# One decoder layer on one core: the last down product and norms token-major, sums in idle work space, steps in a new order

## The chip, the core and the metric

The kernel runs on one core of a Trainium2 chip. Five engines with queues of their own work side by side: TensorE (PE, its weight loads PEld), VectorE (DVE), ScalarE (ACT), GpSimd (POOL) and SyncE (SP), which issues most transfers. Each takes its instructions in the order in which they stand in its queue and waits there for semaphores. The metric is the device time of one execution, in microseconds (us); lower is better.

## The reference

One layer of a hybrid decoder on 1024 prompt tokens and 32 sample tokens (T = 1056), width D = 1024, all in float32:

```python
proj = x @ w_in                                   # split among four head groups
...
mix = jnp.concatenate([o_a, o_b, o_c, o_d], axis=-1) @ w_o
x = layer_norm(ALPHA * x + mix, ln1_g, ln1_b)
x = layer_norm(ALPHA * x + memory_attention(x, mem_k, mem_v, w_xq, w_xo), ln2_g, ln2_b)
ffn = (jax.nn.silu(x @ w_gate) * (x @ w_up)) @ w_down
x = layer_norm(ALPHA * x + ffn, ln3_g, ln3_b)
```

The feed-forward width is 2816, that is 22 tiles of 128 or 11 pairs. Besides x the layer returns new caches and states, which the change does not touch. The change lies in the feed-forward part and the last norm.

## The kernel before, in words

**Numbers.** A float32 product is made of three passes in a faster type: each factor is split into a high part (a ScalarE cast, L206) and a low part (the difference, on VectorE or GpSimd, L214), and `mm3` (L198 to L202) adds high·high, high·low and low·high. Names end in h and l for the two parts: `Xh`, `Xl` are the input, `wh`, `wl` a weight, `dh`, `dl` a down weight, `hh`, `hl` or `he` the product silu(gate)·up. The weights' parts of gate and up live in rings of two buffers, `WH` and `WL`. Raw weights arrive by transfers of 512 KB into `rw`. Many smaller tiles share general slots, taken by `H(...)` and returned by `free(...)`.

**Layout.** Activations are feature-major: `M` has 128 features by 8 tiles by 1056 tokens. Products go to PSUM tiles, `PM` (3 buffers, pm) and `PSB` (5 buffers, ps).

**Feed-forward.** The tokens go in two halves, 0 to 512 and 512 to 1056 (`PART`; widths 256+256 and 272+272). Some pairs of the first half are run early, beside cross-attention (`ff_early`). For the others each pair has seven products in place of eight (`products`, L1624): sums of weight quarters (`sc`, `s4` in the tile `work`) and of token quarters, which `sums_a` makes for the first half and `sums_b` (L1593) for the second. `half_gate`, `half_up` and `half_down` each yield after a product or a group, and `play(ORDER..., streams)` interleaves them: one letter is one step of that stream. `half_down(hf, p)` loads two down weights, then has 16 groups (8 feature tiles by 2 token ranges) of 6 matmuls, each drained by a VectorE add into `M` (L1744). The first pair of the second half is run without sums (`gate_up(ff, PART[1])`), and `sums_b()` follows it.

**Last norm.** `finish(i)` (L1756) takes a block of 128 tokens (block 8: the 32 sample tokens): 8 transposes of `M` to token-major PSUM (`tp`, L220), `bn_stats` (L1765) and `bn_aggr` (L1766), subtraction of the mean and gain (L1772), `rsqrt` (L222: a logarithm, an exponential and one step of refinement), then by mode either a VectorE row that scales and adds the bias (mode 0, L1781) or a ScalarE scale and a GpSimd add (mode 1, L1787), then the store (L1789). Blocks 0 to 3 run beside pairs 1 to 4 of the second half, blocks 4 to 8 at the very end beside the down product of the last pair, in which the token ranges come in the order 784-1056, 640-784, 512-640.

**Tables.** ScalarE's Silu and its Exp/Ln lie in different function tables. `act` (L152) puts an explicit load (L156) ahead of an Exp or Ln, behind the last Silu recorded; where the queue comes out otherwise, the compiler adds a load at L159 or L160.

**Order.** The program is recorded in the order of the code and the strings, and then a scheduler with a timeline model orders each engine's queue. So a string moves instructions only in part; the rows below show what came out.

Of the kernel before, what the change touches and what calls it, by code (L numbers as in the profile page):

```python
# [91 lines left out]
def build(ctx: ExitStack, tc: tile.TileContext, A):  # L92
# [58 lines left out]

    def act(out, in_, func, **kw):  # L152
        if func in (AF.Exp, AF.Ln):
            if table["set"] != "ln_exp":
                with tc.issue_after(table["last"]) if table["last"] else nullcontext():
                    table["load"] = S.preload_act_table_set("natural_log_exp_and_others").ins  # L156
                table["set"] = "ln_exp"
            with tc.issue_after(table["load"]):
                return S.activation(out, in_, func, **kw)  # L159
# [59 lines left out]
    def tp(out, in_, n=P):  # L219
        PE.transpose(out, in_, ident[:n, :n])  # L220

    def rsqrt(y, v, eps, t):  # L222

        V.tensor_scalar(t, v, eps, None, ALU.add)
# [4 lines left out]
        V.scalar_tensor_tensor(y, t, 1.5, y, ALU.add, ALU.mult)
# [1363 lines left out]
    def sums_b():  # L1593

        (a0, a1), (b0, b1) = PART[1]
        places = [lambda t, i: t[:, 2 * i:2 * i + 2, b0:b1], lambda t, i: t[:, 2 * i:2 * i + 2, 0:272],
                  lambda t, i: t[:, 4 + 2 * i:6 + 2 * i, 0:272],
                  lambda t, i: t[:, 4 * i:4 * i + 4, 272:408].rearrange("p (k s) n -> p k s n", s=2)]
        for i in range(2):
# [4 lines left out]
            V.tensor_tensor(t2, M[:, j, b0:b1], t1, ALU.subtract)  # L1604
            V.tensor_tensor(t4, M[:, j, a0:a1], t2, ALU.subtract)
            for n, (x, e) in enumerate(((t1, V), (t2, V), (t3, G), (t4, V))):
                h, l = places[n](Xh, i), places[n](Xl, i)
                if n == 3:
                    x = x.rearrange("p k (s n) -> p k s n", s=2)
                S.copy(h, x)  # L1610
                e.tensor_tensor(l, x, h.bitcast(F32), ALU.subtract)
            free(t1, t2, t3, t4)
# [81 lines left out]
    def half_up(hf, p):
        if p - 1 in downs[hf]:
            need(f"d{hf}.{p - 1}")
        sl = sil_of(hf)
# [8 lines left out]

        def hl(m):
            S.copy(hs[m][0], sl[:, m])
# [47 lines left out]
    def finish(i):  # L1756

        gb = gbt[0]
        n = P if i < 8 else NB * TS
        st, ag = SM([P, 2, 6], s="fst", tag="fst", bufs=2), SM([P, 5], s="fag", tag="fag", bufs=2)  # L1760
        pss = [PM(), PM()] if CFG['fpm'] and i >= 4 else [PSB(), PSB()]
        for hf in range(2):
            for f in range(4):
# [1 line left out]
            V.bn_stats(st[:n, hf], pss[hf][:n])  # L1765
        V.bn_aggr(ag[:n, 0:2], st[:n])  # L1766
        y = H([P, D], s="y")
        hs = [slice(0, 512), slice(512, D)]
        mode = CFG['fin'].get(i, 0)
        if mode < 2:  # L1770
            for hf in range(2):
                V.scalar_tensor_tensor(y[:n, hs[hf]], pss[hf][:n], ag[:n, 0:1], gb[0][:n, hs[hf]], ALU.subtract, ALU.mult)  # L1772
# [86 lines left out]
```

## Time and profile before

| what | value |
|---|---|
| time, median of 3 runs | 1430.63 us (1429.28 to 3872.03) |
| the profiled execution, its time | 1430.61 us |
| its span (first to last instruction) | 1428.8 us |
| mean granted TensorE clock | 0.973 |
| HBM read, written | 125.32 MB, 6.78 MB |

The 40 slices of the span, each digit the busy share in tenths:

```profile
PE   6999999998998998799999999999899999999995
...
DVE  6704658589667768687487999887688898888866
ACT  4424753432556758666346443443434553343334
POOL 5222452364000001022052000001400000000001
PEclk9999999999899999899999999999999999999997
```

TensorE is nearly full in all but the first and the last slice, about 36 us each. The slices near 28 (1000 to 1036 us) hold the first pair of the second half, the last two the tail. A row of a timeline has the start in us, the duration in us, the engine, line, operation, tiles and shape, and in brackets the idle time of that engine just before and what ended it. A row of a wait has total us, number and longest.

### The profile page before, as it was taken

Reading aid. Unit: us, or ns where it says so; the run is one execution under the profiler, and the core shown is the slowest. Engines: PE = TensorE matmul, PEld = TensorE weight load, DVE = VectorE, ACT = ScalarE, POOL = GpSimd, SP = SyncE. Lnnn points to the kernel's source line nnn. Section 1 sums busy time; section 2 is a strip of 40 time slices with the busy share of each in tenths; the row PEclk is TensorE's granted clock in tenths of the full one; section 3 lists DMA queues with packets and bytes.
Section 4 is the critical chain, followed back from the end, with each engine's and each line's share of the span. In section 5 each row is a group of like instructions: output and inputs, shape, how many; then the busy total and the mean of one; then the engine's idle time right before and its main releaser. Section 6 shows DMA issues by size and latency. Waiting matters only on the chain.

```text
span 1428.8 us, 25133 instructions
## 1 busy us (share of the span) xinstructions
PE 1345.6 (94%) x10065; PEld 1279.2 (90%) x10065; DVE 1077.6 (75%) x1972; ACT 670.0 (47%) x1147; POOL 236.4 (17%) x164
## 2 busy tenths in 40 slices
PE   6999999998998998799999999999899999999995
PEld 5998888997897997688799999999799998999995
DVE  6704658589667768687487999887688898888866
ACT  4424753432556758666346443443434553343334
POOL 5222452364000001022052000001400000000001
PEclk9999999999899999899999999999999999999997
DMA  9201111110253445143422333332333333333311
GB/s 301 77 21 41 31 30 50 47 40 24 75 163 104 148 119 151 49 126 119 133 60 68 110 104 104 90 118 75 111 97 91 102 104 112 100 100 90 104 60 63
DMA packets 188447, 132.61 MB, mean 93 GB/s; under 512 B 14573, under 2 KB 177618, under 8 KB 188306
## 3 DMA queue, kind: packets, MB, share of 16 engines
q1 hardware_dynamic: 187225, 128.27, 29.9%
q0 software_dynamic: 928, 2.67, 0.6%
q8 instruction: 79, 1.29, 0.4%
q14 instruction: 39, 0.31, 0.1%
q10 hardware_dynamic: 176, 0.07, 0.0%
HBM read 125.32 MB, written 6.78 MB: 92 GB/s over the span
## 4 chain that ended last, share of the span: by engine, by line
PE 41%; DVE 7%; DMA 4%; ACT 3%; issue 2%; POOL 0%; DVEq 0%; ACTq 0%; POOLq 0%; SPq 0%
PE ps L199 7%; PE ps L202 7%; PE ps L200 7%; PE pm L199 6%; PE pm L200 6%; PE pm L202 6%; DMA rw<-in_w_gate 2%; DVE wl L214 1%; DMA rw<-in_w_up 1%; PE ps L1313 1%; ACT L159 1%; ACT dh L206 1%; DMA rw<-in_w_down 0%; PE ps L1358 0%; DVE M L1481 0%
## 5 line engine op out<-in xcount | busy, mean ns | idle before, releaser
L199 PE MATMUL pm<-Xh,wh 128*128 128x256 f32 (+3 forms) x944 | 270.6, 310 | 14.7 <-ACT Xh L1133 9.8
L200 PE MATMUL pm<-Xl,wh 128*128 128x256 f32 (+3 forms) x944 | 267.2, 306 | 3.4 <-DVE Xl L1134 1.9
L206 ACT CAST wh<-rw 128x1024 fp32r<-128x1024 f32 x145 | 151.8, 1050 | 154.0 <-PE pm L200 43.7
L199 PEld LDWEIGHTS pm<-Xh,wh 128*128 128x128 f32 x944 | 180.8, 192 | 21.5 <-ACT Xh L1133 11.4
L214 DVE TENSOR_TENSOR wl<-rw,wh 128x1024 fp32r<-128x1024 f32 x122 | 152.8, 1254 | 49.3 <-ACT wh L206 46.3
L200 PEld LDWEIGHTS pm<-Xl,wh 128*128 128x128 f32 x944 | 180.7, 192 | 7.2 <-issue 2.5
L202 PE MATMUL pm<-Xh,wl 128*128 128x256 f32 (+3 forms) x944 | 159.4, 305 | 0.0
L202 PEld LDWEIGHTS pm<-Xh,wl 128*128 128x128 f32 x944 | 139.7, 191 | 1.5 <-issue 1.2
L199 PE MATMUL ps<-hh,dh 128*128 128x272 f32 (+3 forms) x370 | 99.9, 291 | 15.3 <-ACT dh L206 8.1
L214 POOL TENSOR_TENSOR wl<-rw,wh 128x1024 fp32r<-128x1024 f32 x23 | 57.1, 2482 | 287.0 <-ACT wh L206 269.3
L200 PE MATMUL ps<-hh,dh 128*128 128x272 f32 (+3 forms) x370 | 99.1, 286 | 0.0
L199 PEld LDWEIGHTS ps<-hh,dh 128*128 128x128 f32 x370 | 70.2, 191 | 17.4 <-ACT dh L206 8.6
L206 ACT CAST dh<-rw 128x1024 fp32r<-128x1024 f32 x44 | 45.9, 1047 | 82.1 <-PE ps L202 27.0
L1744 DVE TENSOR_TENSOR M<-M,ps 128x272 f32<-128x272 f32 (+3 forms) x175 | 69.7, 412 | 12.4 <-PE ps L202 12.0
L199 PE MATMUL ps<-Xh,wh 128*128 128x272 f32 (+1 forms) x296 | 76.5, 287 | 0.0
L200 PE MATMUL ps<-Xl,wh 128*128 128x272 f32 (+1 forms) x296 | 76.4, 287 | 0.0
L202 PE MATMUL ps<-hh,dl 128*128 128x272 f32 (+3 forms) x370 | 75.8, 285 | 0.0
L200 PEld LDWEIGHTS ps<-hh,dh 128*128 128x128 f32 x370 | 70.2, 190 | 0.4 <-DVE hh L1709 0.4
L199 PE MATMUL pm<-mixh,wh 128*128 128x256 f32 (+1 forms) x256 | 65.9, 291 | 0.2 <-ACT mixh L160 0.2
L200 PE MATMUL pm<-mixl,wh 128*128 128x256 f32 (+1 forms) x256 | 65.4, 289 | 0.2 <-DVE mixl L1168 0.2
L199 PE MATMUL pm<-hh,dh 128*128 128x272 f32 (+3 forms) x222 | 60.8, 291 | 3.8 <-DVE y L1772 2.3
L206 ACT CAST g<-work 128x1024 fp32r<-128x1024 f32 x34 | 35.7, 1049 | 60.1 <-PE pm L200 26.2
(454 smaller groups left out, 3668.9 us busy)
## 6 DMA issues: line engine op xcount, KB each, us to landing
rw<-in_w_gate SPq DMA_DIRECT2D x45, 512.0 KB
rw<-in_w_up SPq DMA_DIRECT2D x44, 512.0 KB
rw<-in_w_down SPq DMA_DIRECT2D x44, 512.0 KB
rw<-in_w_o SPq DMA_DIRECT2D x23, 384.0 KB
rw<-in_w_in SPq DMA_DIRECT2D x15, 512.0 KB
xraw<-in_x_prompt SPq DMA_DIRECT2D x8, 512.0 KB
out_y_prompt<-y SPq DMA_DIRECT2D x8, 512.0 KB
vreg<-in_w_o SPq DMA_DIRECT2D x9, 384.0 KB
```

The lines of the kernel that those rows point to most:

```text
L159: return S.activation(out, in_, func, **kw)
L199: PE.matmul(out, wh(k), xh(k), start=(start and k == 0), stop=False)
L200: PE.matmul(out, wh(k), xl(k), start=False, stop=False)
L202: i = PE.matmul(out, wl(k), xh(k), start=False, stop=(k == nk - 1))
L206: S.copy(hi, raw)
L214: (e or G).tensor_tensor(lo, raw, hi.bitcast(F32), ALU.subtract)
L1313: PE.matmul(sc_ps[r0:r0 + 64, :256], zq[:, 2 * b + ft], kx[:, b - b0, ft], start=(b % 4 == 0 and ft == 0), stop=(b % 4 == 3 and ft == 1))
L1744: V.tensor_tensor(z, z, ps, ALU.add)
```

## The change

1. **Tail.** The down product of the last pair is no longer run feature-major. `finish(4)` to `finish(8)` compute it token-major, with the hidden activations as the stationary and the down weight, 512 wide, as the moving operand, and add `M` itself by four plain float32 matmuls with the identity in place of the four transposes. Per block that is 2 × (6 + 4) matmuls. The 144 matmuls and 24 adds of the old product and 40 transposes go; 60 matmuls 512 wide and 40 of the identity come. The weights are loaded and split at the end of the last `play` ("w"), into the ring `WH`/`WL`. The order is 4, 5, 6, 7, 8; modes of 4 and 5 change from 0 to 1, of 8 from 1 to 0. The sample output is stored in two halves on two queues.
2. **rsqrt** is cut in two: the sum and the two ScalarE functions stand ahead of the gain rows in `finish`, the refinement behind.
3. **Tables.** The explicit load comes behind the last four Silu recorded, not the last one.
4. **sums_b.** Its temporaries lie in idle parts of `work` instead of four general slots at a time, all its VectorE and GpSimd rows are on VectorE, and it runs in three steps between the tiles of the pair without sums. That pair's weight splits and low parts of `hh` go from GpSimd to VectorE.
5. **ORDER1, 2, 4, 5 and 6** have new strings. `half_up` asserts that its gate has been recorded.

```diff
-CFG = {... 'fin': {0: 0, 1: 1, 2: 1, 3: 1, 6: 1, 7: 1, 8: 1, 4: 0}, ...}
+CFG = {... 'fin': {0: 0, 1: 1, 2: 1, 3: 1, 6: 1, 7: 1, 8: 0, 4: 1, 5: 1}, ...}
-ORDER3 = "ddddddddd87dddd8877dddd56dddddddd5566"
-ORDER4 = "gggdggddggddggddddddddddddduuuuuuuuu"
-ORDER5 = "gggdggddggddggddddfddddddddduuuufuuuuu"
-ORDER6 = "gggggggggduuuuuuuuuddddddddddddddddd"
+ORDER3 = "444555666777888"
+ORDER4 = "ggdgggdggddddggdddddddddddduuuuuuuuu"
+ORDER5 = "gggdgdgddggdddddfddddggddddduuuufuuuuu"
+ORDER6 = "ggggggggguuuuuuuuuddddddddddddddddddw"
...
         if func in (AF.Sigmoid, AF.Silu):
-            table["set"], table["last"] = "other", i.ins
+            table["set"], table["last"] = "other", [*table["last"], i.ins][-4:]
...
-            G.tensor_tensor(hl[:, t0 - o:t1 - o], t, hh[:, t0 - o:t1 - o].bitcast(F32), ALU.subtract)
+            (V if t0 == 512 or t0 == 784 else G).tensor_tensor(hl[:, t0 - o:t1 - o], t, hh[:, t0 - o:t1 - o].bitcast(F32), ALU.subtract)
...
+        t1 = [room(2368), room(2912)]
         for i in range(2):
             k, j = slice(2 * i, 2 * i + 2), slice(4 + 2 * i, 6 + 2 * i)
-            t1, t2, t3, t4 = [H([P, 2, 272], s="tq") for _ in range(4)]
-            V.tensor_tensor(t1, M[:, k, b0:b1], M[:, k, a0:a1], ALU.subtract)
-            G.tensor_tensor(t3, M[:, j, b0:b1], M[:, k, b0:b1], ALU.subtract)
+            t2, t3, t4 = [room(736 + 544 * n) for n in range(3)]
+            V.tensor_tensor(t1[i], M[:, k, b0:b1], M[:, k, a0:a1], ALU.subtract)
+            V.tensor_tensor(t2, M[:, j, b0:b1], t1[i], ALU.subtract)
+            cut(t2, i, 1)
+            V.tensor_tensor(t3, M[:, j, b0:b1], M[:, k, b0:b1], ALU.subtract)
...
-    def half_down(hf, p, order=None):
+    def down_weights(p, ring=False):
         d = []
         for ff in (2 * p, 2 * p + 1):
             r = RX().rearrange("p a b -> p (a b)")
             nc.sync.dma_start(r, w_d[ff * P:(ff + 1) * P, :])
-            d.append(split(r, H([P, D], F32R, s="dh"), H([P, D], F32R, s="dl"), V))
+            d.append(split(r, *((WH([P, D]), WL([P, D])) if ring else (H([P, D], F32R, s="dh"), H([P, D], F32R, s="dl"))), V))
+        return d
...
-        pss = [PM(), PM()] if CFG['fpm'] and i >= 4 else [PSB(), PSB()]
+        pss = [PM(), PM()] if i in (4, 6, 8) else [PSB(), PSB()]
         for hf in range(2):
-            for f in range(4):
+            for f in () if d else range(4):
                 tp(pss[hf][:n, f * P:(f + 1) * P], M[:, 4 * hf + f, i * P:i * P + n])
+            if d:
+
+                cs = slice(i * P - 512, i * P - 512 + n)
+                hs = slice(hf * 512, hf * 512 + 512)
+                for k in range(2):
+                    for x in range(2):
+                        PE.matmul(pss[hf][:n], flat[k][x][:, cs], d[k][0][:, hs], start=(k == 0 and x == 0), stop=False)
+                for k in range(2):
+                    PE.matmul(pss[hf][:n], flat[k][0][:, cs], d[k][1][:, hs], start=False, stop=False)
+                for f in range(4):
+                    PE.matmul(pss[hf][:n, f * P:(f + 1) * P], M[:, 4 * hf + f, i * P:i * P + n], ident, start=False, stop=(f == 3))
...
-        gate_up(ff, PART[1])
-    xs_[1] = quarters(1) + sums_b()
+        gate_up(ff, PART[1], V)
+        run(sb, 1)
+    run(sb, 99)
```

**Rows, ScalarE's queue at the first pair of the second half, before** (sil: silu of the gate; tq: the sums' temporaries in general slots; dh: the two down weights of the last pair of the first half, of which the first is cast some rows above):

```order
L1445 CAST hh_10422<-sil_10552 128x272
L1610 CAST Xh<-tq_10668 128x2x272
L1445 CAST hh_10422<-sil_10579 128x272
L1610 CAST Xh<-tq_10684 128x2x272
L1610 CAST Xh<-tq_10685 128x2x272
L1610 CAST Xh<-tq_10686 128x2x272
L206 CAST g_967_7814<-work 128x1024
L206 CAST wh_10858<-rw_10845 128x1024
L206 CAST dh_10708<-rw_10706 128x1024
```

and now:

```order
L208 CAST dh_10694<-rw_10692 128x1024
L1612 CAST Xh<-work 128x2x272
L1454 CAST hh_10420<-sil_10457 128x272
L208 CAST dh_10700<-rw_10698 128x1024
L162 ACTIVATE sil_10562<-pm_10563 128x272
L1612 CAST Xh<-work 128x4x136
L208 CAST wh_10840<-rw_10836 128x1024
L162 ACTIVATE sil_10589<-pm_10590 128x272
L1454 CAST hh_10422<-sil_10562 128x272
```

The second cast of a down weight stood behind the last casts of hh and four casts of sums; now both stand ahead of the second tile's first hh.

**TensorE's queue near 582 us, where cross-attention and early feed-forward work are interleaved, before** (mkv, qx: keys and queries of the scores; he, dh: a down product of the first half; Xh, wh: gate products that need this step's new x):

```order
L1124 MATMUL ps_5509<-vreg,cf 128x256
L1237 MATMUL ps_5594<-mkv,qx_5527 128x256
L1237 MATMUL ps_5595<-mkv,qx_5527 128x256
...
L199 MATMUL pm_5776<-Xh,wh_5765 128x256
L199 MATMUL pm_5818<-Xh,wh_5771 128x256
L220 MATMUL ps_5610<-cf,px_5592 128x128 x4
```

and now:

```order
L1133 MATMUL ps_5509<-vreg,cf 128x256
L1246 MATMUL ps_5594<-mkv,qx_5517 128x256
L1246 MATMUL ps_5595<-mkv,qx_5517 128x256
L201 MATMUL ps_5609<-he_5195,dh_5480 128x256
L202 MATMUL ps_5609<-he_5195,dh_5480 128x256
L201 MATMUL ps_5609<-he_5364,dh_5486 128x256
L202 MATMUL ps_5609<-he_5364,dh_5486 128x256
L204 MATMUL ps_5609<-he_5195,dl_5481 128x256
```

Eight such groups of down matmuls (48 in all), which stood behind the first Xh matmuls, now stand ahead of them.

**ScalarE's queue in the tail, before** (fag: mean, variance and rsqrt of a block; y: the block's output):

```order
L159 ACT_TABLE_LOAD
L159 ACTIVATE fag_14976<-fag_14976 32x1
L159 ACT_TABLE_LOAD
L159 ACTIVATE fag_14976<-fag_14976 32x1
L160 ACTIVATE y_14990<-y_14990,fag_14976 32x1024
```

and now, from the last table load on:

```order
L158 ACT_TABLE_LOAD
L208 CAST wh_14896<-rw_14894 128x1024
L1730 CAST hh_14616<-work 128x544
L1730 CAST hh_14618<-work 128x544
L161 ACTIVATE fag_14904<-fag_14904 128x1 x2
L162 ACTIVATE y_14930<-y_14930,fag_14904 128x1024
```

Each logarithm and each exponential of the tail had a table load of its own, ten in all; now one load stands ahead of all of them.

More of the change, by code (lines that the diff above doesn't have):

```diff
@@ L147, in PSB @@
         return pp.tile([P, 512], F32, name=nm(s), tag="psb", bufs=5)
-    table = {"set": None, "last": None, "load": None}
+    table = {"set": None, "last": [], "load": None}
     def act(out, in_, func, **kw):
@@ L154, in act @@
             if table["set"] != "ln_exp":
-                with tc.issue_after(table["last"]) if table["last"] else nullcontext():
+                with ExitStack() as es:
+                    for i in table["last"]:
+                        es.enter_context(tc.issue_after(i))
                     table["load"] = S.preload_act_table_set("natural_log_exp_and_others").ins
@@ L222, in rsqrt, with rsqrt_a, rsqrt_b @@
     def rsqrt(y, v, eps, t):
+        rsqrt_a(y, v, eps, t)
+        return rsqrt_b(y, t)
+    def rsqrt_a(y, v, eps, t):
         V.tensor_scalar(t, v, eps, None, ALU.add)
         act(y, t, AF.Ln)
-        i = act(y, y, AF.Exp, scale=-0.5)
+        table["e"] = act(y, y, AF.Exp, scale=-0.5)
+    def rsqrt_b(y, t):
+        i = table["e"]
         V.tensor_tensor(t, y, t, ALU.mult)
@@ L1598, in sums_b, with cut, room @@
                   lambda t, i: t[:, 4 * i:4 * i + 4, 272:408].rearrange("p (k s) n -> p k s n", s=2)]
+        def cut(x, i, n):
+            h, l = places[n](Xh, i), places[n](Xl, i)
+            if n == 3:
+                x = x.rearrange("p k (s n) -> p k s n", s=2)
+            S.copy(h, x)
+            V.tensor_tensor(l, x, h.bitcast(F32), ALU.subtract)
+        def room(o):
+            return work[:, o:o + 544].rearrange("p (k n) -> p k n", k=2)
+        t1 = [room(2368), room(2912)]
         for i in range(2):
             k, j = slice(2 * i, 2 * i + 2), slice(4 + 2 * i, 6 + 2 * i)
-            t1, t2, t3, t4 = [H([P, 2, 272], s="tq") for _ in range(4)]
-            V.tensor_tensor(t1, M[:, k, b0:b1], M[:, k, a0:a1], ALU.subtract)
-            G.tensor_tensor(t3, M[:, j, b0:b1], M[:, k, b0:b1], ALU.subtract)
[L1604 to L1612, printed above, removed]
+            t2, t3, t4 = [room(736 + 544 * n) for n in range(3)]
[3 more added lines that the diff above has]
+            V.tensor_tensor(t3, M[:, j, b0:b1], M[:, k, b0:b1], ALU.subtract)
+            cut(t3, i, 2)
+            V.tensor_tensor(t4, M[:, j, a0:a1], t2, ALU.subtract)
+            cut(t4, i, 3)
+            yield
+        for i in range(2):
+            cut(t1[i], i, 0)
         ks = [lambda t, k: t[:, k, b0:b1], lambda t, k: t[:, k, 0:272], lambda t, k: t[:, 4 + k, 0:272],
               lambda t, k: t[:, 2 * k:2 * k + 2, 272:408]]
-        return [tuple((lambda k, t=t, f=f: f(t, k)) for t in (Xh, Xl)) for f in ks]
+        xs_[1] = quarters(1) + [tuple((lambda k, t=t, f=f: f(t, k)) for t in (Xh, Xl)) for f in ks]
+        yield
     def quarters(hf):
@@ L1692, in half_gate @@
         yield from products(hf, w_g, p, result)
+        flags.add(f"g{hf}.{p}")
     def half_up(hf, p):
+        need(f"g{hf}.{p}")
         if p - 1 in downs[hf]:
@@ L1730, in half_down @@
             nc.sync.dma_start(r, w_d[ff * P:(ff + 1) * P, :])
-            d.append(split(r, H([P, D], F32R, s="dh"), H([P, D], F32R, s="dl"), V))
+            d.append(split(r, *((WH([P, D]), WL([P, D])) if ring else (H([P, D], F32R, s="dh"), H([P, D], F32R, s="dl"))), V))
+        return d
+    def half_down(hf, p, order=None):
+        hs, tiles = hx.pop((hf, p))
+        d = down_weights(p)
         o = PART[hf][0][0]
@@ L1754, in load_gb, with finish @@
             nc.gpsimd.dma_start(t, A[n].to_broadcast([P, D]))
-    def finish(i):
+    def finish(i, d=None, flat=None):
         gb = gbt[0]
@@ L1760, in finish @@
         st, ag = SM([P, 2, 6], s="fst", tag="fst", bufs=2), SM([P, 5], s="fag", tag="fag", bufs=2)
-        pss = [PM(), PM()] if CFG['fpm'] and i >= 4 else [PSB(), PSB()]
+        pss = [PM(), PM()] if i in (4, 6, 8) else [PSB(), PSB()]
         for hf in range(2):
-            for f in range(4):
+            for f in () if d else range(4):
                 tp(pss[hf][:n, f * P:(f + 1) * P], M[:, 4 * hf + f, i * P:i * P + n])
+            if d:
[8 more added lines that the diff above has]
+                    PE.matmul(pss[hf][:n, f * P:(f + 1) * P], M[:, 4 * hf + f, i * P:i * P + n], ident, start=False, stop=(f == 3))
+                if not hf:
+                    yield
             V.bn_stats(st[:n, hf], pss[hf][:n])
         V.bn_aggr(ag[:n, 0:2], st[:n])
+        if d:
+            yield
         y = H([P, D], s="y")
@@ L1769, in finish @@
         mode = CFG['fin'].get(i, 0)
+        rsqrt_a(ag[:n, 2:3], ag[:n, 1:2], LN_EPS, ag[:n, 3:4])
         if mode < 2:
@@ L1772, in finish @@
                 V.scalar_tensor_tensor(y[:n, hs[hf]], pss[hf][:n], ag[:n, 0:1], gb[0][:n, hs[hf]], ALU.subtract, ALU.mult)
-        rsqrt(ag[:n, 2:3], ag[:n, 1:2], LN_EPS, ag[:n, 3:4])
+        rsqrt_b(ag[:n, 2:3], ag[:n, 3:4])
         if mode > 1:
@@ L1789, in finish @@
             nc.sync.dma_start(A["y_prompt"][0, i * P:(i + 1) * P, :], y)
+        elif mode == 0:
+            for hf in range(2):
+                (nc.sync, nc.scalar)[hf].dma_start(A["y_sample"].rearrange("b t d -> (b t) d")[:, hs[hf]], y[:n, hs[hf]])
         else:
@@ L1820, in build, with wlast @@
             free(*gbs)
-    play(ORDER6, {"g": half_gate(1, p + 1), "u": half_up(1, p + 1), "d": half_down(1, p)})
+    d = []
+    def wlast():
+        d.extend(down_weights(NP - 1, True))
+        yield
+    play(ORDER6, {"g": half_gate(1, p + 1), "u": half_up(1, p + 1), "d": half_down(1, p), "w": wlast()})
     free(*g3t)
@@ L1824, in build @@
     load_gb([gb2[:, 0], gb2[:, 1]])
-    dn = half_down(1, NP - 1, [(f, r) for r in ((784, T), (640, 784), (512, 640)) for f in range(KD)])
-    play(ORDER3, {"d": dn, **{str(i): finish(i) for i in (4, 5, 6, 7, 8)}})
+    hs, tiles = hx.pop((1, NP - 1))
+    flat = [tuple(t.rearrange("p c n -> p (c n)") for t in x) for x in hs]
+    play(ORDER3, {str(i): finish(i, d, flat) for i in (4, 5, 6, 7, 8)})
+    free(*tiles)
 _INS = ["x_prompt", "x_sample", "cache_swa_k", "cache_swa_v", "state_hgrn", "state_conv", "state_pool",
```

8 lines of the change are left out of this document (4 added, 4 removed).

## The prediction

> **What bounds the kernel now.** I read the page first, then TensorE's waits, then windows and timelines around the longest waits and the end. The page:
>
> ```profile
> PE 1345.6 (94%) x10065; PEld 1279.2 (90%) x10065; DVE 1077.6 (75%) x1972; ACT 670.0 (47%) x1147; POOL 236.4 (17%) x164
> ...
> PE 41%; DVE 7%; DMA 4%; ACT 3%; issue 2%; POOL 0%; DVEq 0%; ACTq 0%; POOLq 0%; SPq 0%
> ```
>
> TensorE is the bound, with 1428.8 − 1345.6 = 83 us idle. So a change pays in three ways: less TensorE work, an idle stretch filled, or a shorter end after the last matmul. TensorE's waits, as total us, times and longest:
>
> ```profile
> PE pm L199 <- ACT Xh L1133: 9.8, 2, 8.5
> PE ps L199 <- ACT dh L206: 8.1, 2, 7.1
> ...
> PE ps L199 <- ACT hh L1708: 5.1, 3, 2.4
> ...
> PE pm L220 <- DVE y L1772: 2.6, 1, 2.6
> ...
> PE pm L199 <- DVE y L1772: 2.3, 1, 2.3
> ```
>
> The 8.5, the 7.1 and the last two (4.9) stand where the change edits. Idle also costs clock afterwards. The windows give length, busy us of TensorE, its loads, VectorE, ScalarE and GpSimd, then the granted clock:
>
> ```profile
> 582.00:590.40 8.40, 0.00 (x0) 0.00 (x0) 6.77 (x13) 5.76 (x16) 0.00 (x0) 0.73 0.19 56
> 590.40:596.20 5.80, 5.77 (x24) 4.51 (x25) 4.26 (x7) 5.51 (x10) 0.00 (x0) 0.50 0.00 0
> ...
> 1029.10:1033.00 3.90, 3.86 (x18) 3.86 (x19) 3.90 (x5) 1.06 (x2) 0.00 (x0) 0.50 0.71 254
> ...
> 1412.00:1419.00 7.00, 4.60 (x21) 4.15 (x20) 4.87 (x17) 5.62 (x8) 0.85 (x2) 0.50 0.37 150
> ```
>
> Behind each of the two long waits, and through the end, TensorE runs at 0.50.
>
> **The tail.** These rows price it (start, duration):
>
> ```profile
> 1387.01 0.39 PE L199 MATMUL ps<-hh,dh 128*128 128x272 f32 x1 [1.01 <-ACT dh L206]
> ...
> 1387.49 0.29 PE L200 MATMUL pm<-hh,dh 128*128 128x272 f32 x1
> ...
> 1389.01 0.28 PE L200 MATMUL pm<-hh,dh 128*128 128x272 f32 x1
> ...
> 1417.67 1.27 PE L220 MATMUL pm<-cf,M 128*128 128x128 f32 x5
> ...
> 120.76 0.34 PE L199 MATMUL pm<-Xh,wh 128*128 128x384 f32 x1
> ...
> 121.99 0.34 PE L200 MATMUL pm<-Xl,wh 128*128 128x384 f32 x1
> ...
> 321.77 1.06 PE L471 MATMUL ps<-R,gl 128*128 128x128 f32 x8
> ...
> 323.73 1.50 PE L471 MATMUL ps<-R,gl 128*128 128x128 f32 x12
> ```
>
> The matmuls of the pair before end at 1387.01 − 1.01 = 1386.0. The 144 matmuls and 40 transposes that follow end at 1417.67 + 1.27 = 1418.94, 33 us, much of it idle or at half clock. The new tail has 5 blocks, each of 12 matmuls 512 wide and 8 plain f32 ones 128 wide against the identity. No row has 512 columns in the split type, so I work from start to start: 272 columns take (1389.01 − 1387.49)/12 = 0.127 us, 384 take (121.99 − 120.76)/7 = 0.176, so 0.00044 a column and 0.232 at 512. A plain f32 matmul leaves two records (L471 is 64 matmuls in the program and 128 records in the trace), and four more records cost 1.50 − 1.06 = 0.44, so one matmul is 0.22. A block is 12 × 0.232 + 8 × 0.22 = 4.54 us, five are 22.7: about what the old instructions need without waits (144 × 0.127 + 40 × 0.11 = 22.7 at most), but in one piece. The weights come into the ring of the gate and up weights while the previous pair's matmuls run, so the 1.0 us wait goes and TensorE ends at 1386.0 + 22.7 = 1408.7.
>
> VectorE must keep up, and the end behind the last matmul counts in full. Its rows, last block before:
>
> ```profile
> 1418.98 0.70 DVE L1765 BATCH_NORM_STATS2 fst<-pm 128x6 f32<-128x512 f32 x1 [0.15 <-PE pm L220]
> 1419.72 0.21 DVE L1766 BATCH_NORM_AGGREGATE fag<-fst 128x2 f32<-128x12 f32 x1
> 1419.96 1.41 DVE L1772 SCALAR_TENSOR_TENSOR y<-pm,fag,gb 128x512 f32<-128x512 f32 x2
> ...
> 1421.68 1.28 ACT L159 ACT_TABLE_LOAD   x1
> ...
> 1423.60 0.16 DVE L229 SCALAR_TENSOR_TENSOR fag<-fag 128x1 f32<-128x1 f32 x1
> 1423.79 1.42 DVE L1781 SCALAR_TENSOR_TENSOR y<-y,fag,gb 128x512 f32<-128x512 f32 x2
> ```
>
> Per block VectorE has 2 × 0.70 + 0.21 + 1.41 + 4 × 0.16 = 3.7 us, below 4.54, so TensorE sets the pace; the 24 M adds of this product are gone. The end before is 1428.8 − 1418.94 = 9.86. In the new order the small sum and the logarithm stand ahead of the 1.41 us pair and run beside it, and the 1.28 us table load is gone: 0.15 + 0.70 + 0.26 + 0.19 + 1.41 + 0.58 + 1.42 = 4.7 to the last VectorE row (each with its gap). Then at most 1428.8 − 1425.2 = 3.6 for a store that falls from 512 to 64 KB; I take 2.6. That makes 7.3, and 1416.0 as the end: **−12.8**. Block 7's GpSimd add and 512 KB store end about 0.6 us ahead of that (the add 7.6 behind its block's matmuls, plus 3.6; block 8 ends at 4.54 + 7.3). Bounds: if the f32 matmuls cost one record (0.11), VectorE's 3.7 sets the pace, 18.5 for five, −17; if each block is late by 1 us, −8. The weights' splits are the same instructions, only earlier.
>
> The Trainium skill, TensorE: Matmul & The Clock Gate, section Back-to-back issue gap, gives about 131 ns for a sustained 512-column matmul; by that a block would be 3.35 us and the sum 5 us lower. The rows speak against it: 384 columns already take 176 ns here, so I stay with 0.232.
>
> **Sums of quarters.** Rows around the 7.1 us wait:
>
> ```profile
> 1029.14 0.58 PE L199 MATMUL ps<-hh,dh 128*128 128x256 f32 x1 [7.12 <-ACT dh L206]
> ...
> 1028.05 1.04 ACT L206 CAST dh<-rw 128x1024 fp32r<-128x1024 f32 x1
> ...
> 1026.79 1.86 DVE L1605 TENSOR_TENSOR tq<-M,tq 128x544 f32<-128x544 f32 x1
> ...
> 1029.18 0.71 DVE L1611 TENSOR_TENSOR Xl<-tq,Xh 128x544 fp32r<-128x544 f32 x1
> ...
> 996.00:1022.00 26.00, 26.00 (x209) 25.82 (x207) 12.81 (x17) 11.13 (x19) 13.18 (x9) 1.00 0.27 81
> ```
>
> The second down weight's cast waits for an H slot that the sums' temporaries hold. With these in work space, both casts stand ahead of the second tile's first hh cast. Gone are 7.1 of idle and, behind it, up to half of 3.9 us at 0.50, of which I take 1.8. Sum **−8.9**. VectorE takes over from GpSimd 4 weight splits (4 × 1.22, below), 4 splits of hl (about 0.4 each, half as wide as the 0.71 row), 2 differences and 2 low parts (4 × 0.71): 9.3 us. In the 26 us ahead VectorE is busy 12.8, so 22.1 of 26 covers them, without the 1.86 that stood beside a GpSimd row. If it falls behind there, the wait returns: bound 0, and below −8.9 only the rest of the half clock, −9.1. The gb loads on GpSimd's queue move past nothing that waits.
>
> **The 8.5 us wait.** It ends with a chain over VectorE and ScalarE:
>
> ```profile
> 585.47 1.22 DVE L214 TENSOR_TENSOR wl<-rw,wh 128x1024 fp32r<-128x1024 f32 x1 [1.49 <-ACT wh L206]
> ...
> 590.43 0.80 PE L199 MATMUL pm<-Xh,wh 128*128 128x256 f32 x2 [8.51 <-ACT Xh L1133]
> ```
>
> The new order puts 8 groups of 6 down matmuls ahead of those that need Xh: 48 × 0.120 (256 columns by the line above) = 5.8 us of work that stood later. Their 8 drains (0.4 each) go into VectorE's 1.49 idle and otherwise delay Xh, up to 2 us. The half clock of 590–596 (up to 2.9 lost) shrinks if the idle left, about 3, is short enough. I take **−6**; bounds −2 (drains delay Xh, clock falls as before) and −8.7.
>
> **Other layout.**
>
> ```profile
> 306.00:316.00 10.00, 7.38 (x56) 6.55 (x55) 9.92 (x13) 3.35 (x4) 7.12 (x6) 1.00 0.19 56
> ...
> 627.00:984.00 357.00, 348.05 (x2831) 334.42 (x2830) 293.57 (x554) 166.17 (x278) 39.10 (x24) 1.00 0.33 99
> ...
> 1081.40:1118.00 36.60, 34.16 (x274) 33.94 (x273) 33.10 (x62) 15.61 (x20) 2.40 (x1) 1.00 0.31 90
> ...
> 1258.90:1292.00 33.10, 33.10 (x266) 33.10 (x265) 28.80 (x55) 12.42 (x16) 0.00 (x0) 1.00 0.32 97
> ...
> 1111.33 3.35 DVE L214 TENSOR_TENSOR wl<-rw,wh 128x1024 fp32r<-128x1024 f32 x1
> ```
>
> At 306 TensorE is idle 2.6 of 10 us, but VectorE is busy 9.92, so another order of matmuls gains little: **−2**, bounds −5 and +3. The same holds for the four second-half steps with norms in them (36.6 us against 33.1 without): VectorE is busy 33.1 of 36.6, and one split takes 3.35 beside the 2.4 us GpSimd add. **0**, bounds ±4. Fewer table loads are hidden there, ScalarE being busy 15.6. From 627 to 984 TensorE is busy 348 of 357: **0**, ±3.
>
> Sum: −12.8 − 8.9 − 6 − 2 = −29.7. The profiled execution took 1430.61 (its span 1428.8), the median of the runs is 1430.63: 1430.6 − 29.7 = **1401 us**, −2.1%.
>
> **Rivals.**
> 1. The dh wait only changes its holder: VectorE is late with the sums, and the 8.9 stay: 1410. For it: 9.3 us more on VectorE. Against: 13 of 26 us idle.
> 2. The tail is paced by VectorE behind GpSimd. Four 128-row blocks now end in a GpSimd add, two before. The 3.35 shows a two-input VectorE row held while GpSimd adds; the small rsqrt rows are such rows, and if each block waits out a 2.4 us add, it takes 3.7 + 2.4 = 6.1, so 5 × 1.6 = 8 more: 1409. By my times the add ends 7.6 behind its block's matmuls and the next block's first such row comes at 7.3, so 0.3 a block. The Trainium skill, SBUF — State Buffer, section Who interferes with whom, states such a lock between GpSimd and a VectorE row with two SBUF inputs; by that rule, the trace agrees (3.35 against 1.22).
> 3. Faster: the low bounds of the tail and of the 8.5 wait hold: 1430.6 − 17 − 8.9 − 8.7 − 2 = 1394.
> 4. Slower. In the nine steps with the new second-half layout the first down matmul is recorded one gate product earlier (12 matmuls, 1.5 us), while its hh is cast late. Before, hh made TensorE wait three times, 2.4 at most. If a step waits 2.4 + 1.5 and loses 1.7 to the clock behind it, it costs 5.6; from six such steps on (34) the gain of 29.7 is eaten: 1435, and 1452 with nine. Against: the five steps without a norm have no wait at all (33.10 busy of 33.10).
> 5. The change does little: only the tail pays, 1418, as the two long waits move elsewhere.
>
> **How the numbers follow.** Forecast 1396–1407: 0.50. Rival 1 (1410): 0.13. Rival 2 (1409): 0.10. Rival 3 (1394): 0.12. Rival 4 (1435): 0.04. Rival 5 (1418): 0.11. The range 1389 to 1416 leaves out rival 4, most of 5 and the ends of 3. A change of 2%, to 1402.0, is about what a measurement can tell. Of the forecast's 0.50, 0.37 lies below 1402; with rival 3 that is 0.49 faster. Rivals 1, 2, 5, most of 4 and the rest of the forecast are the same, 0.49; slower by 2% (over 1459) 0.02.
>
> **What would show it.** Tail: the last matmul 23 us behind the last M add's group, blocks 4.5 us apart, no table load in it, 7.3 us to the end, clock near 1. Sums: no wait for dh near 1022 and no GpSimd row there. The 8.5 wait: 3 us or less. It is wrong if VectorE passes 9 tenths around 1000–1030, if 512-wide matmuls start over 0.25 apart, or if new waits for hh appear in the second half.

## The result, and the profile after

The changed kernel takes 1396.26 us (median of 4 runs, 1394.24 to 1397.13) against 1430.65 before; the ratio is 0.9761, 95% interval 0.9742 to 0.9780. One run of the kernel before, 3872.03 us, stands far outside; without it the median is 1430.63. The change makes the kernel 34.4 us faster; 29.7 were forecast. The profiled execution took 1397.13 us, its span is 1395.4. Three rows of the page after (busy time, granted clock in 40 slices, chain that ended last):

```profile
PE 1339.8 (96%) x10021; PEld 1271.8 (91%) x10021; DVE 1070.0 (77%) x1958; ACT 653.1 (47%) x1134; POOL 219.3 (16%) x153
...
PEclk9999999999998999999999999999999999999999
...
PE 21%; DVE 3%; DMA 2%; issue 1%; ACT 0%; DVEq 0%; SPq 0%
```

TensorE's idle time went from 83.2 to 1395.4 − 1339.8 = 55.6 us, and its busy time fell by 5.8 us. TensorE's waits after (total us, times, longest):

```profile
PE ps L222 <- DMA mkv<-in_emb_ln_b: 5.8, 1, 5.8
PE ps L1111 <- DVE vreg L1101: 5.6, 1, 5.6
PE ps L222 <- DVE px L1254: 4.0, 3, 2.3
PE ps L480 <- DVE R L470: 3.3, 2, 3.1
PE ps L201 <- DVE M L1488: 2.9, 2, 1.8
...
PE ps L201 <- ACT hh L1730: 1.2, 2, 0.9
```

The 8.5 us for Xh, the 7.1 for dh and the waits for y are gone, and hh fell from 5.1 to 1.2. New are 4.0 for px (it was 1.2) and 2.9 for `M` at L1488, the drains of early down products.

To see where the time went, I cut both spans at the same matmuls of the program, counted by kind (the 673rd matmul with hh, for one, starts at 1046.70 and at 1030.00 us), and took the differences of those starts. This table is worked out from the two traces:

| stretch (span before, us) | before | after | gain | TensorE idle (tail: up to its last matmul) | at 0.50 |
|---|---|---|---|---|---|
| up to 341 | 341.4 | 341.8 | −0.4 | | |
| 341–393, attention (ORDER1) | 52.0 | 44.7 | 7.3 | 3.6 → 0.1 | 13.7 → 3.4 |
| 393–521 | 128.0 | 129.4 | −1.4 | 7.5 → 8.2 | 6.8 → 10.2 |
| 521–792, with the 8.5 us wait (ORDER2) | 270.6 | 270.7 | −0.1 | 23.7 → 19.8 | 13.7 → 13.7 |
| 792–964 | 171.7 | 171.3 | 0.4 | 1.2 → 0.6 | 0 → 0 |
| 964–1047, with the sums | 82.9 | 72.0 | 10.9 | 7.1 → 0 | 6.8 → 0 |
| 1047–1259, steps with norms | 212.2 | 207.4 | 4.8 | 6.8 → 3.3 | 3.4 → 0 |
| 1259–1374 | 114.9 | 115.8 | −0.9 | 0 → 0 | 0 → 0 |
| 1374 to the end, tail | 55.0 | 42.1 | 12.9 | 7.4 → 0 | |

Two rows are not the same work on both sides. The new strings put 12 matmuls behind the end of the stretch with the sums (611 in its window before, 599 after) and so into 1259–1374. In e7 and e10 below, with the old strings and the new sums, that stretch takes 73.4 us and 1259–1374 takes 114.7. So 9.5 of the 10.9 us belong to the sums, 1.4 to these matmuls, and the loss of 0.9 in 1259–1374 is theirs too.

The windows show some of these stretches, first before, then after (length, busy us and instructions of TensorE, its loads, VectorE, ScalarE and GpSimd, granted clock, transfers). Before:

```profile
341.40:393.40 52.00, 48.37 (x278) 40.45 (x277) 36.18 (x66) 23.08 (x41) 10.40 (x5) 0.87 0.21 58
579.30:634.30 55.00, 46.18 (x365) 42.66 (x364) 39.25 (x70) 34.74 (x73) 7.34 (x4) 0.91 0.29 87
963.80:1046.70 82.90, 75.78 (x611) 75.39 (x610) 58.73 (x102) 29.86 (x44) 20.41 (x14) 0.96 0.32 98
1046.70:1258.90 212.20, 205.39 (x1615) 203.52 (x1614) 190.56 (x359) 92.20 (x116) 7.72 (x3) 0.99 0.33 99
```

After:

```profile
341.80:386.60 44.80, 44.75 (x278) 37.16 (x277) 37.05 (x72) 23.60 (x44) 10.46 (x5) 0.96 0.24 67
575.60:629.80 54.20, 48.61 (x365) 44.34 (x364) 40.57 (x73) 36.91 (x78) 7.53 (x4) 0.94 0.30 88
958.00:1030.00 72.00, 72.00 (x599) 72.00 (x597) 62.02 (x113) 29.74 (x44) 1.14 (x2) 1.00 0.36 108
1030.00:1237.40 207.40, 204.06 (x1618) 202.28 (x1617) 188.04 (x360) 88.60 (x113) 7.21 (x3) 1.00 0.34 103
1365.20:1388.50 23.30, 23.27 (x142) 18.91 (x141) 14.49 (x38) 6.22 (x12) 7.18 (x4) 1.00 0.17 69
1388.50:1395.40 6.90, 0.00 (x0) 0.00 (x0) 4.10 (x10) 0.41 (x2) 2.33 (x1) 0.84 0.27 95
```

In the sums' stretch GpSimd fell from 20.4 to 1.1 busy us, VectorE rose by only 3.3, and TensorE is busy 72.00 of 72.00. The last two rows are the tail: 23.3 us without a gap at full clock, then 6.9 to the end.

### The profile page after: what moved, and what is told of

It is laid out like the page before. It is cut to its first block, busy times and chain, and to the rows that moved or that the text cites. A ratio compares the mean times of both kernels' runs of the same rounds, so it can differ in the third digit from the quotient of the medians.

```text
span 1395.4 us, 24975 instructions
## 1 busy us (share of the span) xinstructions
PE 1339.8 (96%) x10021; PEld 1271.8 (91%) x10021; DVE 1070.0 (77%) x1958; ACT 653.1 (47%) x1134; POOL 219.3 (16%) x153
## 5 line engine op out<-in xcount | busy, mean ns | idle before, releaser
L202 PE MATMUL pm<-Xl,wh 128*128 128x256 f32 (+3 forms) x944 | 271.0, 309 | 3.2 <-DVE Xl L1143 1.9
L216 DVE TENSOR_TENSOR wl<-rw,wh 128x1024 fp32r<-128x1024 f32 x128 | 158.3, 1239 | 42.3 <-ACT wh L208 38.8
L201 PE MATMUL ps<-hh,dh 128*128 128x272 f32 (+1 forms) x340 | 91.5, 288 | 3.1 <-DVE M L1770 1.6
L202 PE MATMUL ps<-hh,dh 128*128 128x272 f32 (+1 forms) x340 | 90.5, 285 | 0.0
L204 PE MATMUL ps<-hh,dl 128*128 128x272 f32 (+1 forms) x340 | 69.1, 285 | 0.0
L1770 DVE TENSOR_TENSOR M<-M,ps 128x272 f32<-128x272 f32 (+1 forms) x160 | 65.1, 421 | 4.5 <-PE ps L204 4.5
L201 PEld LDWEIGHTS ps<-hh,dh 128*128 128x128 f32 x340 | 63.8, 188 | 4.6 <-DVE M L1770 2.2
L202 PEld LDWEIGHTS ps<-hh,dh 128*128 128x128 f32 x340 | 63.9, 188 | 0.0
L201 PEld LDWEIGHTS ps<-Xh,wh 128*128 128x128 f32 x296 | 55.7, 188 | 0.8 <-DVE M L1768 0.8
```

What stands on the lines that cost most here:

```text
L201: PE.matmul(out, wh(k), xh(k), start=(start and k == 0), stop=False)
L202: PE.matmul(out, wh(k), xl(k), start=False, stop=False)
L204: i = PE.matmul(out, wl(k), xh(k), start=False, stop=(k == nk - 1))
L216: (e or G).tensor_tensor(lo, raw, hi.bitcast(F32), ALU.subtract)
L1770: V.tensor_tensor(z, z, ps, ALU.add)
```

## The experiments

Each kernel is the changed one with one part undone, unless the diff says more. Times are medians of 4 runs; "stretch" is a row of the table above, cut at the same matmuls. They ran in three groups (e1 to e4, e5 to e8, e9 to e12), in which the kernel before took 1431.08, 1428.61 and 1429.65 us, so a difference of 2 us between medians of two groups is not clear. The stretches with an edit in them repeat better: 44.7 to 44.8 us for 341–393 in every kernel with the new ORDER1, 72.0 for the sums' stretch in all eight with the new sums and the new ORDER4 to 6, and 42.1 to 42.4 for the new tail with the cut rsqrt, the new table rule and the M matmuls.

**e1, old tail.**

```diff
...
-    play(ORDER3, {str(i): finish(i, d, flat) for i in (4, 5, 6, 7, 8)})
...
+    dn = half_down(1, NP - 1, [(f, r) for r in ((784, T), (640, 784), (512, 640)) for f in range(KD)])
+    play(ORDER3, {"d": dn, **{str(i): finish(i) for i in (4, 5, 6, 7, 8)}})
```

> The changed kernel with the old tail: the last pair's down product feature-major, transposes, old order and modes; the new table rule stays. Theory (the token-major order takes out waits, half clock and the long end): the whole 12.7 us that the traces show for this stage come back, 1409 us (1407 to 1412), and at the half-clock rows the end is near 0.5. Rival (the ten table loads were what slowed the old tail, and the table rule alone removes them): at most 4 us come back, 1397 to 1400.

Measured 1404.57 us, 8.3 above the changed kernel: between the two forecasts. **e11, old tail and old table rule.**

```diff
-            table["set"], table["last"] = "other", [*table["last"], i.ins][-4:]
+            table["set"], table["last"] = "other", [i.ins]
```

> The changed kernel with the old tail and the old table rule. Theory (the 12.7 us of the tail are 8.3 for the token-major product and some 4.4 for table loads, which the old tail needs again): 1407 to 1411, ten table loads in the tail. Rival (the loads are hidden in the old tail too): 1403 to 1406.

Measured 1406.06 us (ratio 0.9843, 0.9817 to 0.9869), at the upper edge of the rival's range: by the medians the loads add 1.5 us to the old tail, not 4.4. By stretches the tail takes 55.0 us before, 52.6 in e11, 50.5 in e1 and 42.1 in the changed kernel. So, undone in this order, 8.4 of the 12.9 are the token-major product with its order, 2.1 the table rule, and the 2.4 between the kernel before and e11 were not taken apart (both experiments keep the cut rsqrt). The windows of e1's tail and its end:

```profile
1365.40:1395.10 29.70, 24.45 (x184) 22.95 (x184) 25.07 (x65) 6.29 (x13) 4.71 (x2) 0.91 0.10 38
1395.10:1403.10 8.00, 0.00 (x0) 0.00 (x0) 4.17 (x10) 0.43 (x3) 2.34 (x1) 0.50 0.35 141
```

The old form keeps 5 us of idle and a clock of 0.91, even with no table load in it.

**e4, old table rule alone** (the diff of e11, with the new tail).

> The changed kernel with the old table rule (the explicit load only behind the last Silu recorded). Theory (fewer table loads gave the 4.8 us between 1065 and 1240 us, in the steps with norms): 1400 to 1402, with some ten automatic loads back. Rival (the loads are hidden, and the new step order gave them): 1396 to 1397.5.

Measured 1399.56 us, 3.3 above. The steps with norms take 208.4 us instead of 207.4, as they do in e8, which keeps the new rule; the loss lies at the end. ScalarE's last rows in e4 (start, duration):

```profile
1391.93 1.28 ACT L161 ACT_TABLE_LOAD   x1
1393.22 0.20 ACT L161 ACTIVATE fag<-fag 32x1 f32<-32x1 f32 x1
1393.44 1.28 ACT L161 ACT_TABLE_LOAD   x1
1394.73 0.20 ACT L161 ACTIVATE fag<-fag 32x1 f32<-32x1 f32 x1
```

Ten loads are back in the tail, and the last block's two stand on the path behind the last matmul: 10.1 us to the end instead of 6.9. One more is back ahead of the tail and none in the steps with norms, which have 8 here as in the changed kernel and 11 in the kernel before. So the rule pays at the end; whether three loads fewer gave something in the steps with norms, as the theory has it, e4 could not show.

**e2, old sums of quarters.** General slots, some rows on GpSimd, all behind the pair.

```diff
...
-        gate_up(ff, PART[1], V)
-        run(sb, 1)
-    run(sb, 99)
+        gate_up(ff, PART[1])
+    xs_[1] = quarters(1) + sums_b()
```

> The changed kernel with the old sums of quarters (general slots, some rows on GpSimd, after the pair) and GpSimd splits in that pair. Theory (the sums held the slot of a down weight): a wait for dh of about 7 us returns near 1010 us of the span and the time is 1405 to 1408. Rival (the gain of 11 us there came from the new step order, or the wait only changes its holder): 1396 to 1400, with no wait for dh above 2 us.

Measured 1401.89 us, 5.6 above (the forecast range began at 1405). TensorE's wait in e2:

```profile
PE ps L201 <- ACT dh L208: 7.1, 1, 7.1
```

It is the old wait, to the tenth. The stretch takes 81.6 us instead of 72.0, so 9.7 come back there (with the rounding of the starts): 7.1 of idle, and 2.6 of TensorE's busy time (74.6 instead of 72.0). The profiled execution makes up 5.1 of them ahead of the stretch, where TensorE's order is the same in both kernels: 1.9 up to 341, 2.6 from 341 to 792 and 0.5 from there on. From 521 to 792 it spends 3.4 us at half clock, the changed kernel 13.7.

**e5, slots alone, and e6, GpSimd alone.** In e5 the temporaries are general slots again, in its second step five at a time (the first `t1` is kept until the end) where the kernel before held four. In e6 they stay in `work`, but the GpSimd rows are back.

```diff
...
-            t2, t3, t4 = [room(736 + 544 * n) for n in range(3)]
+            t1.append(H([P, 2, 272], s="tq"))
+            t2, t3, t4 = [H([P, 2, 272], s="tq") for _ in range(3)]
```

```diff
...
-            V.tensor_tensor(t3, M[:, j, b0:b1], M[:, k, b0:b1], ALU.subtract)
+            G.tensor_tensor(t3, M[:, j, b0:b1], M[:, k, b0:b1], ALU.subtract)
...
-        gate_up(ff, PART[1], V)
+        gate_up(ff, PART[1])
```

> The changed kernel, its sums again in general slots (four at a time), but all on VectorE and in the same three steps. Theory (the slot is what the down weight waited for): the wait for dh of some 7 us near 1010 us is back, 1401 to 1406. Rival (GpSimd's share of the sums, and what it held up on VectorE, made the wait): no wait for dh above 2 us, 1395 to 1398.

> The changed kernel with its sums in the idle work space, but a difference and a low part of each pass on GpSimd, and the weight splits and low parts of hh of that pair on GpSimd, as before. Theory (the slot alone matters): no wait for dh above 2 us, 1395 to 1398. Rival (the engine matters): a wait of 4 to 8 us there, 1400 to 1405.

Measured 1405.12 us (e5, in the theory's range) and 1399.75 us (e6, between both, with runs from 1396.47 to 1403.83; the median is not clear of the changed kernel's). The stretch is 78.9 us in e5 and 77.5 in e6, against 72.0 with neither and 81.6 with both. TensorE's waits that are back, first in e5, then in e6:

```profile
PE ps L201 <- ACT hh L1731: 4.1, 2, 3.8
...
PE ps L201 <- ACT dh L208: 3.9, 1, 3.9
```

```profile
PE pm L201 <- DVE sil L1453: 3.2, 3, 2.1
```

In e5 it is the wait for the down weight, 3.9 us instead of 7.1, and one of 3.8 for hh in the next stretch, which takes 209.8 us. In e6 no wait for dh is left, as its theory has it; TensorE waits for VectorE, late with the products of gate and up (2.7 of the 3.2 us in this stretch). So neither theory nor rival holds alone: in this stretch the slot costs 6.9, the engine 5.5, and both together 9.7. Rows of VectorE and GpSimd in e6 show how the engine costs:

```profile
997.03 2.82 DVE L1613 TENSOR_TENSOR Xl<-work,Xh 128x544 fp32r<-128x544 f32 x1
999.89 1.76 DVE L1627 TENSOR_TENSOR work<-M,work 128x544 f32<-128x544 f32 x1
1001.58 0.71 DVE L1613 TENSOR_TENSOR Xl<-work,Xh 128x544 fp32r<-128x544 f32 x1
```

```profile
996.54 2.74 POOL L216 TENSOR_TENSOR wl<-rw,wh 128x1024 fp32r<-128x1024 f32 x1 [2.29 <-ACT wh L208]
999.24 1.83 POOL L1613 TENSOR_TENSOR Xl<-work,Xh 128x544 fp32r<-128x544 f32 x1
```

The VectorE row that takes 0.71 us by itself takes 2.82 beside GpSimd's 2.74 and ends 0.6 behind it; the next one waits out the following GpSimd row in the same way. Work given to GpSimd here did not relieve VectorE, it stopped it: VectorE is busy 62.9 us in the stretch in e6, with 101 rows, and 62.0 in the changed kernel, with 113.

**e3, old ORDER1.**

```diff
-ORDER1 = "MIMMIIIMIIVIIIVVICMMIMVTIVIIIVTVVVTTTTTTTSTSTSTTTSTSSTTTSAAASSATATAAATTTTTAAAAATAAATATSSATTTTSBBTTTBTTSTTABBBBBBBTTBTBTTBTBBTBBBBBBBTBTTTTTTBTBBBBPTTTTTTP"
+ORDER1 = "MIMMIIIMIIVIVIIIVCMMIMIVVVTTIIIVVVTTTTTTTSTSSTTSTSTSTTTTSAAASSATATAAAATTTTTAAAAATAAATATSSASTTTTTTSBBTTTBBTTABBBBBBBTTTBTTTBBBBTBBBBBBBBTTTTPTTTTBBBBBPTTTTTT"
```

> The changed kernel with the old ORDER1 string. Theory (ORDER1 gave the 7 us that the traces show between 341 and 394 us, by a shorter half-clock stretch): 1402 to 1404. Rival (VectorE paces that stretch and the string is worth 2 us at most, the rest follows from other parts): 1396 to 1399.

Measured 1403.05 us, 6.8 above, as the theory has it. The stretch is 51.7 us again. Window of the stretch in e3, and TensorE's wait there:

```profile
341.00:392.80 51.80, 48.17 (x278) 40.25 (x278) 36.18 (x66) 23.09 (x41) 10.40 (x5) 0.87 0.21 58
```

```profile
PE ps L596 <- DVE Sb L566: 3.6, 3, 1.7
```

The three waits for a state of the recurrence stand between 348 and 354 us. The half clock begins with the last of them and lasts 13.7 us, in which TensorE works; in the kernels with the new string the waits are gone and 3.4 us at half clock are left.

**e8, old ORDER2.**

```diff
-ORDER2 = "XXWWXXWWXWWWWWNNWWWNNWNXNNNWNWWN00NXNNNNW0WWW0NWN00WW0WW00W00WNNWN1NNN1W11NNNWWW1NNF1F1NNN11NNNNF1WW1FNNNNNN2NN22FF2NN22NNNNFNNF2FF2FN2FFNN2F233NN3FNF33FNFFNFN33N3F3NF3F3FN3F33F33F33333N33FFFFFFFFFNNNNNNNNN"
+ORDER2 = "XXWWXXWWXWWWWWNNWWWNNWNXNNNWNWWN00NXNNNNW0WWW0NWN00WW0WW00W00WNNWN1NNN1W11NNNWWW1NNF1F1NNN11NNNNF1WW1FNNNNNNNN2222NNFF22NNNNFNNF2FF2FN2FFNN2F233NN3FNF33FNFFNFN33N3N3F3N3F3FF33F33F33333FN3F3FFFNFFFFNNNNNNNN"
```

> The changed kernel with the old ORDER2 string. Theory (the 48 down matmuls ahead of the Xh matmuls fill the 8.5 us wait near 575 us): the wait of 7 to 9 us is back there and the time is 1399 to 1403. Rival (what was filled is lost again to half clock, as the four stretches at 0.5 between 555 and 617 us of the changed kernel hint): the wait is back, but the time is 1395 to 1398.

Measured 1395.20 us, not slower. TensorE's wait in e8 is back:

```profile
PE pm L201 <- ACT Xh L1142: 9.8, 2, 8.3
...
PE ps L222 <- DVE px L1254: 1.2, 1, 1.2
```

The rival's forecast holds: the wait costs nothing on balance. From 521 to 792 e8 takes 269.7 us, the changed kernel 270.7, the kernel before 270.6. The wait for px is back at 1.2, and the one for `M` is gone. That half clock took back what was filled, as the rival has it, is not shown: TensorE's idle time there is 22.7 us in e8 and 19.3 to 22.1 in the kernels with the new string, so little was filled on balance.

**e7, old ORDER4, 5 and 6; e9, uncut rsqrt; e10, both.** The expectations of e9 and e10 name the old table rule too, but the kernels that ran keep the new one: their diffs hold the rsqrt and, in e10, the strings alone, and both have 23 table loads like the changed kernel (e4 and e11 have 34).

```diff
-        rsqrt_a(ag[:n, 2:3], ag[:n, 1:2], LN_EPS, ag[:n, 3:4])
...
-        rsqrt_b(ag[:n, 2:3], ag[:n, 3:4])
+        rsqrt(ag[:n, 2:3], ag[:n, 1:2], LN_EPS, ag[:n, 3:4])
```

> The changed kernel with the old ORDER4, ORDER5 and ORDER6 strings (the weights of the last product still loaded at the end of ORDER6). Theory (the new second-half order gave the 4.8 us that the traces show between 1065 and 1240 us, with waits for hh gone): 1399 to 1402, and two or three waits for hh of 1 to 2.5 us are back. Rival (they follow from the table rule or from the sums): 1395 to 1397.5.

> The changed kernel with the uncut rsqrt behind the gain rows and the old table rule (the table rule alone gave 1399.6). Theory (the cut rsqrt shortens VectorE's wait for ScalarE and gave most of the 4.8 us in the steps with norms, and 0.7 us at the end): the stage of the four steps is 210 to 213 us long instead of 207.5, 1402 to 1405 in all. Rival (the stage does not depend on it): that stage stays at 206 to 209, 1399 to 1401.

> As the kernel with the uncut rsqrt and the old table rule, and the old ORDER4, ORDER5 and ORDER6 besides: all that the change edits for the steps with norms is undone. Theory (these three together hold the 4.8 us): the stage is 211 to 213 us long, as before, with waits for hh near 2.4 us. Rival (the stage is shorter since it starts in another state, behind the new sums): 206 to 209.

Measured 1393.95, 1398.88 and 1399.01 us (e10 from 1396.31 to 1403.04). The steps with norms take 207.0, 208.4 and 210.6 us. e7 lies below both of its forecasts and is not slower than the changed kernel, so by themselves the strings gain nothing that the runs show. e9's steps are in its rival's range, e10's between theory and rival. In the kernels that leave strings and rsqrt alone the stretch varies from 206.3 to 208.4 us (209.8 in e5, with the wait of 3.8 us), so neither part alone brings the old stretch back. Both undone bring 3.2 of 4.8 in one profile, 2.2 us above the highest of that scatter, and the old wait exactly, as e10's row shows:

```profile
PE ps L201 <- ACT hh L1730: 5.1, 3, 2.4
```

This wait is 1.8 in e7, 2.1 in e9 and 1.2 in the changed kernel. So the new order and the cut rsqrt each suffice to remove most of it. The other 1.6 us stay open: the kernel before has 11 table loads in these steps, all later ones have 8, and no run has the old table rule together with the old strings and the uncut rsqrt. At the end e9 takes 7.5 us behind the last matmul instead of 6.9, which is what the cut rsqrt is worth there.

**e12, no M in the tail.**

```diff
...
-                for f in range(4):
-                    PE.matmul(pss[hf][:n, f * P:(f + 1) * P], M[:, 4 * hf + f, i * P:i * P + n], ident, start=False, stop=(f == 3))
```

> The changed kernel without the 40 matmuls of the last norms' five blocks that add M by the identity: the residual is left out of these blocks. Theory (TensorE paces the tail at 4.54 us a block, of which 1.78 are these; without them VectorE's 3.7 us would be the pace): a block each 3.6 to 3.9 us and 3 to 5 us less in all, 1391 to 1393.5. Rival (VectorE or the PSUM buffers pace the tail already): 1395 to 1397.

Measured 1396.94 us (1394.72 to 1400.14): nothing gained, as in the rival. TensorE's part of the tail is 7.3 us shorter (28.0 instead of 35.3 from the 1537th matmul with hh to the last), but the end behind it is 13.5 instead of 6.9. VectorE and GpSimd in e12's tail:

```profile
1377.38 1.84 DVE L236 TENSOR_TENSOR fag<-fag 128x1 f32<-128x1 f32 x1
...
1389.13 2.26 DVE L237 SCALAR_TENSOR_TENSOR fag<-fag 32x1 f32<-32x1 f32 x1
1391.43 0.15 DVE L238 SCALAR_TENSOR_TENSOR fag<-fag 32x1 f32<-32x1 f32 x1
```

```profile
1376.81 2.39 POOL L1827 TENSOR_TENSOR y<-y,gb 128x1024 f32<-128x1024 f32 x1 [14.53 <-ACT fag L161]
...
1386.75 4.64 POOL L1827 TENSOR_TENSOR y<-y,gb 128x1024 f32<-128x1024 f32 x2 [3.42 <-ACT y L162]
```

Rows of one element per partition, 0.15 us by themselves, take 1.84 and 2.26: they end with GpSimd's adds (1379.20 and 1391.39). TensorE's matmuls set the tail's pace in the changed kernel, but the chain over VectorE and GpSimd is only just behind.

## Why the prediction came out, step by step

**Tail, forecast −12.8, measured −12.9.** The rows answer to each price (start and duration, TensorE after):

```profile
1365.27 1.09 PE L1797 MATMUL pm<-wh,hh 128*128 128x512 f32 x4
1366.20 0.62 PE L1799 MATMUL pm<-wl,hh 128*128 128x512 f32 x2
1366.66 1.05 PE L1801 MATMUL pm<-cf,M 128*128 128x128 f32 x8
1367.46 1.17 PE L1797 MATMUL pm<-wh,hh 128*128 128x512 f32 x4
```

Four 512-wide matmuls take 1366.20 − 1365.27 = 0.93, that is 0.233 each (forecast 0.232). Four plain f32 ones leave 8 records, as forecast. The five blocks take 23.2 us (forecast 22.7) and the end 6.9 (forecast 7.3). The figure of 131 ns for a sustained 512-column matmul in the Trainium skill (TensorE: Matmul & The Clock Gate, section Back-to-back issue gap) does not hold for these float32 splits: 233 ns measured. (The prediction's estimate by that page, 5 us lower, comes to 6 by its own terms, 5 × (4.54 − 3.35).) What the forecast did not separate is the share of the parts: the old tail with the new table rule costs 8.3 (e1), the new tail without the rule 3.3 (e4), of which 3.2 stand behind the last matmul.

**Rival 2, GpSimd holding VectorE in the tail.** It did not come, by a narrow margin: 0.3 us a block were forecast. A row of block 7 on VectorE and the add of block 6 on GpSimd, after:

```profile
1386.02 0.28 DVE L236 TENSOR_TENSOR fag<-fag 128x1 f32<-128x1 f32 x1
```

```profile
1383.91 2.38 POOL L1829 TENSOR_TENSOR y<-y,gb 128x1024 f32<-128x1024 f32 x1 [2.20 <-ACT y L162]
```

The small row is 0.13 us longer than by itself and ends with the add at 1386.29; in blocks 5 and 6 such a row is 0.04 and 0.10 longer. In e12, with a shorter block, the same pair costs 1.7 us in block 5 and 2.1 in block 8: the mechanism was right, and only the pace of TensorE kept it off the path.

**Sums, forecast −8.9, measured −9.5** (10.9 in the table, less the 1.4 us of matmuls that moved). The mechanism was right: e2 brings back the same 7.1 us, and rival 1, a wait that changes its holder, did not come. The term for the clock, 1.8, was 0.6 to 0.8 too small: 2.4 us are left beside the 7.1, and 2.6 in e2. Of the 6.8 us at half clock before, 2.9 lay in the wait itself and cost nothing. That VectorE's room was enough "without the 1.86 that stood beside a GpSimd row" was too little said: e6 shows that the GpSimd share alone costs 5.5.

**The 8.5 us wait, forecast −6, measured 0.** The step that failed is "48 × 0.120 = 5.8 us of work that stood later". Before, that work stood between other steps of the same chain. The last of the 48 matmuls starts 12.0 us after the start of the window at 575.6, where it was 23.0 after that at 579.3, but the same 365 instructions take 54.2 us instead of 55.0. Waits for px (4.0) and M (2.9) stand in the place of the long one, in all twelve kernels with the new string (px 4.0 to 4.2, M 2.6 to 2.9). In e8, with the old one, they are 1.2 and none, and it is not slower. The sign that the prediction named, a wait of 3 us or less, did come (2.1), and yet nothing was gained; for this wait it is rival 5, a wait that moves elsewhere.

**ORDER1, forecast −2, measured −7.3.** The step that failed is "VectorE is busy 9.92 of 10, so another order of matmuls gains little". That row is from 306 to 316 us. The loss stood at 349 to 368: 3.6 us of waits, and 13.7 us at half clock, nearly all of them busy. Of the 7.3 us, 3.5 are idle time and 3.6 busy time. I priced the whole from the wrong ten microseconds (e3).

**Steps with norms, forecast 0 ± 4, measured −4.8.** The step that failed is "The same holds", with VectorE's 33.1 of 36.6 us as its reason: 4.8 of the waits for hh of 5.1 us lay in this stretch, and the new order or the cut rsqrt removes most of them (e7, e9, e10). Of "Fewer table loads are hidden there" no run shows the price, as the three loads came back in none.

**Sum.** From −29.7: tail −0.1, sums −0.6, the 8.5 us wait +6.1, ORDER1 −5.3, steps with norms −4.8, the other rows of the table +0.9 together, which gives −33.5, the difference of the spans but for rounding. That the total is near the forecast is in good part luck: a gain that did not come and two that were not seen cancel.

## What to carry to other kernels

Filling a long wait paid nothing here, as the work that filled it had stood between other steps of the same chain: look where it stood before, and whether the chain that ends the stretch gets shorter, not whether the wait vanishes. Short waits ahead of a long run at half clock can cost more than a long wait (7.3 us against none here), so price a stretch by its idle time and its half-clock time, over the whole of both. Work moved from GpSimd to VectorE can be nearly free, where two-input rows of VectorE stand still beside GpSimd's.

## What was not expected of the hardware

With one and the same order of TensorE's instructions from 521 to 792 us, twelve kernels (the changed one and all experiments but e8) take 268.1 to 273.2 us there in their profiled executions, with 3.4 to 13.7 us at 0.50. Where the half-clock stretches fall differs between executions, and so single profiles of two kernels can differ by 5 us in a stretch that is the same in both. So e2 can cost 9.7 us in its own stretch and only 5.6 by its median: part of the difference is made up in stretches with the same order. How much of that is clock was not settled.
